# Reordering the first pair of each group of seven-product matmul pairs, and splitting two SiLU blocks earlier, in a hybrid encoder layer

## The chip, the cores and the metric

The kernel runs on one core of one Trainium2 chip, as one program in one launch. The metric is the device time of an execution in microseconds (us), the median over several executions. The engines are TensorE (PE, matmuls, with its weight loads shown as PEld), VectorE (DVE), ScalarE (ACT), GpSimd (POOL) and SyncE (SP, which issues the weight loads). They run side by side and each takes its own instructions in order.

## What is computed

One layer of a streaming encoder on 640 token rows: a prompt of 512 and 8 samples of 16. Everything is float32.

```
z = x @ w_in                      # columns: xa | ya | glu | q | gates (3 x 1024)
out_a = (rg_lru(conv4(xa)) * gelu(ya)) @ proj_a
out_b = silu(layer_norm(conv31(glu))) @ proj_b
out_c = cross_attention(q, mem_k, mem_v) @ proj_c
merged = g0 * out_a + g1 * out_b + g2 * out_c        # g = sigmoid(gates + b_gate)
x = layer_norm(alpha * x + merged @ w_out)
ffn = (silu(x @ w_ffn_gate) * (x @ w_ffn_up)) @ w_ffn_down   # 2816 wide
x = layer_norm(alpha * x + ffn)
```

## The kernel before

A float32 product is made of three matmuls on rounded operands: every operand is split into a high part (an ACT copy into the rounded type) and a low part (a DVE subtraction of the high part from the original), and hi x hi, hi x lo and lo x hi are added. The function `split` (line 206) is this for one operand. The transposed activations stand in two big tiles, `xh` and `xl`, as eight blocks of 128 features by 640 tokens.

Two groups of weight columns are multiplied by a scheme of seven products in place of eight (Winograd's variant of Strassen's): the eleven-pair FFN part (gate and up projections, all but their first 256 columns) and the last 1024 gate columns. A pair is a 1024 x 256 weight block. Its x operand is cut into four quarters, by feature half and token half: "11", "12", "21", "22" (line 1382). Four sums of quarters are needed too: s1 = 21 + 22, s2 = s1 - 11, s3 = 11 - 21, s4 = 12 - s2. `sums_stream` (line 1386) makes them once for each group, in two blocks of two features each: four adds `xh + xl`, four sums of those, and then the splits of s2, s3, s1, s4. The first group (the gates) writes s1's split in place over quarter 21 of `xh` and `xl`, which no product reads.

`Pair` (line 1429) makes four sums of weight blocks, t1 to t4, on DVE. `seven` (line 1464) issues the products in the order of the table `PRODUCTS` (line 1459): m1 (quarter 11), m6 (s2), m2 (quarter 12), m7 (s3), m5 (s1), m4 (quarter 22), m3 (s4). Each is 12 matmuls of 128 x 320. Four PSUM tiles hold them: m1 and m2 add up in tile x, m6 and m7 in y, m5 and m3 in z, m4 is alone in w. After m1 ACT copies x out; after m6, DVE adds y to that copy; after m7, again; and the four results of a pair are put out after m2, m5, m4 and m3. A product that continues a tile can start only when the earlier value has been read out of it.

The program is recorded step by step (line 1842). A step stands for one product or another block of matmuls. Its weights are rounded (`prep_hi` on ACT, `prep_lo` on DVE) two steps ahead. Before its matmuls its `before` hook runs. After the first part of its matmuls, `advance` lets the side streams (attention, convolutions, the recurrence, the sums) issue instructions as far as a table of prices says that ACT and DVE are free; then pending evacuations are issued. `finish("sums0")` and `finish("sums1")`, the hooks of the second product of each group's first pair (lines 1504 and 1699), issue what is left of the sums.

The down projection follows the FFN pairs. Its left operand is `hT`, 22 blocks of 128 features (the SiLU blocks). `split_h(k)` (line 1701) rounds block k; `before_down` (line 1709), the hook of the first down step, splits blocks 0 and 1, and each step k then splits block k + 2. The weights come in blocks of 1 MB, two at a time; a load starts when the last low half of an older block is made (`Load.take`, line 226).

Of the kernel before, what the change touches and what calls it, by code (L numbers as in the profile page):

```python
# [11 lines left out]
OP = mybir.AluOpType  # L12
# [126 lines left out]
def f32(x):  # L139
    return x.bitcast(F32)  # L140
# [3 lines left out]
def trunk(ctx, tc, x_prompt, x_sample, mem_prompt, state_conv_a, state_lru, state_conv_b, cache_mem_k, cache_mem_v,  # L144
# [171 lines left out]
    def flush():  # L316
        while pending:
            pending.pop(0)()
# [1066 lines left out]

    def sums_stream(in_place=None):

        for n, (t0, k0) in QUARTERS.items():
            quarters[n] = tuple([x[:, k0 + k, t0:t0 + HT] for k in range(half)] for x in (xh, xl))
        parts = {n: ([], []) for n in ("s1", "s2", "s3", "s4")}  # L1390
        last = []
        for i in range(0, half, 2):
            a = {}
            for n, (t0, k0) in QUARTERS.items():
                a[n] = get([128, 2, HT])
                V.tensor_tensor(a[n], *(f32(x[:, k0 + i:k0 + i + 2, t0:t0 + HT]) for x in (xh, xl)), op=OP.add)
                yield "v"
            for out, p, q, op in (("22", "21", "22", OP.add), ("21", "11", "21", OP.subtract),
                                  ("11", "22", "11", OP.subtract), ("12", "12", "11", OP.subtract)):
                V.tensor_tensor(a[out], a[p], a[q], op=op)  # L1400
                yield "v"
            for n, q in (("s2", "11"), ("s3", "21"), ("s1", "22"), ("s4", "12")):
                if n == "s1" and in_place is not None:
                    last.append((i, a[q]))
                    continue
                hi, lo = get([128, 2, HT], F32R), get([128, 2, HT], F32R)
                split(hi, lo, a[q])
                free(a[q])
                sums.extend((hi, lo))
                for to, y in zip(parts[n], (hi, lo)):  # L1410
                    to.extend(y[:, k] for k in range(2))
                yield 1
        if in_place is not None:
            while not in_place():
                yield None
            for i, x in last:
                hi, lo = (y[:, i:i + 2, HT:] for y in (xh, xl))
                split(hi, lo, x)
                free(x)
                yield 1  # L1420
            parts["s1"] = quarters.pop("21")
        quarters.update(parts)

    def sums_over():
        flush()
# [3 lines left out]
    class Pair:  # L1429
# [21 lines left out]
            self.add("t4", "t2", "21", OP.subtract)  # L1451

        def drop(self, n):
            if n in self.t and n != "t2":
                free(self.t.pop(n))
                if n == "t4":
                    free(self.t.pop("t2"))

    PRODUCTS = (("m1", "x", True, "11", "11"), ("m6", "y", True, "s2", "t2"), ("m2", "x", False, "12", "21"),
                ("m7", "y", False, "s3", "t3"), ("m5", "z", True, "s1", "t1"), ("m4", "w", True, "22", "t4"),  # L1460
                ("m3", "z", False, "s4", "22"))
    parity = [0]

    def seven(pair, put, following, begin=None):

        acc, tmp = {}, {}

        def after(n, p):
            if n == "m1":
                tmp["a"], tmp["b"] = get([128, 2, HT]), get([128, 2, HT])  # L1470
                copy(tmp["a"][:, 0], p)
            elif n == "m6":
                V.tensor_tensor(tmp["a"][:, 1], tmp["a"][:, 0], p, op=OP.add)
            elif n == "m2":
                put(0, 0, p, None, None)
            elif n == "m7":
                V.tensor_tensor(tmp["b"][:, 0], tmp["a"][:, 0], p, op=OP.add)
            elif n == "m5":
                put(1, 1, p, tmp["b"][:, 0], OP.add)
            elif n == "m4":  # L1480
                put(0, 1, p, tmp["b"][:, 0], OP.subtract)
                free(tmp["b"])
            else:
                put(1, 0, p, tmp["a"][:, 1], OP.add)
                free(tmp["a"])

        for i, (n, u, opens, xn, wn) in enumerate(PRODUCTS):
            def mm(w, u=u, opens=opens, xn=xn):
                if opens:
                    acc[u] = pu(1)[0][:, :HT]  # L1490
                p = acc[u]
                hi, lo = w
                xhi, xlo = quarters[xn]
                for k in range(half):
                    P.matmul(p, hi[:, k], xhi[k], start=opens and k == 0, stop=False, skip_group_check=not opens)
                    P.matmul(p, hi[:, k], xlo[k], start=False, stop=False, skip_group_check=not opens)
                yield
                for k in range(half):
                    P.matmul(p, lo[:, k], xhi[k], start=False, stop=k == half - 1, skip_group_check=not opens)
                yield  # L1500

            before = None
            if i == 1:
                before = begin
            elif following and i == 2:
                before = following.sums_1
            elif following and i == 3:
# [6 lines left out]
    def pair_steps(pairs, begin=None):  # L1514

        early = steps[-2]
        assert early.before is None
        early.before = lambda: (pairs[0][0].sums_1(), pairs[0][0].sums_2())
        for i, (pair, put) in enumerate(pairs):
            seven(pair, put, pairs[i + 1][0] if i + 1 < len(pairs) else None, begin if i == 0 else None)  # L1520
# [32 lines left out]
    for j in range(KD):  # L1553
# [1 line left out]
    first["pairs"] = len(steps)  # L1555
    pair_steps([(Pair(w_load(w_in, C_G + 128 * j, 7)),
                 through(AF.Sigmoid, lambda i, j=j: slot_of(gates, (0, j + i)), bias=lambda i, j=j: pa[:, j + i, 8:9]))
                for j in range(0, KD, 2)], lambda: finish("sums0"))
    proj_steps(0, proj_a, 8, aT, lambda: (sums_over(), finish("lru", "a")))


# [133 lines left out]
    for m2 in range(2, KF, 2):  # L1695
        pairs.append((Pair(w_load(w_ffn_gate, m2 * 128, 7)),
                      through(AF.Silu, lambda i, m2=m2: slot_of(hT, m2 + i))))
        pairs.append((Pair(w_load(w_ffn_up, m2 * 128, 7)), times(m2)))
    pair_steps(pairs, lambda: finish("sums1"))

    def split_h(k):
        if k < KF:
# [5 lines left out]

    def before_down():
        sums_over()  # L1710
        for k in range(2):
            split_h(k)
        r = one.tile([128, 5, D], F32, name="xres", tag="xh")
        for t in range(5):
            G.dma_start(r[:, t], scratch["x1"][t * 128:(t + 1) * 128, :])
            res[t] = [r[:, t, c * 512:(c + 1) * 512] for c in range(2)]
        g = one.tile([128, 2, D], F32, name="gb2", tag="xl")
        for i, z in enumerate((ln2_g, ln2_b)):
            G.dma_start(g[:, i], bass.AP(tensor=z.tensor, offset=z.offset, ap=[[0, 128], [1, D]]))
        gb["2"] = [[g[:, i, c * 512:(c + 1) * 512] for c in range(2)] for i in range(2)]  # L1720
# [176 lines left out]
```

## Time and profile before

| what | value |
|---|---|
| median of 3 executions | 1102.43 us (1102.43 to 1102.51) |
| the profiled execution: its time, its span | 1102.82 us, 1101.1 us |
| PE busy, weight loads busy | 97%, 91% of the span |
| DVE, ACT, POOL busy | 73%, 44%, 15% |
| mean granted TensorE clock | 0.989 of full speed |

The span runs from the first to the last instruction of the core; the time of the execution is 1.7 us longer. Busy shares are averages over stages with different limits. A row of a timeline gives the start in us from the span's start, the duration, the engine, the operation, output tile, input tiles, their shapes, how many equal instructions in a row stand behind it, and in brackets how long the engine stood idle before it and who ended that. `s` is any slot of the pool (640 floats in each of 128 partitions), `wr` a raw weight block, `wh` and `wl` two buffers that hold rounded weights (in a pair step each holds both halves of one product's weights, by turns), `pu` and `pv` PSUM tiles.

### The profile page before, as it was taken

The page shows a single profiled execution, that of the slowest core. Times are in us where ns is not written, and L with a number is a line of the kernel's source. Part 1 is how long each engine was busy: PE and PEld are TensorE (multiplying, and loading weights), DVE is VectorE, ACT ScalarE, POOL GpSimd, SP SyncE. Part 2 cuts the span into 40 slices and gives each one's busy share as a digit, 9 for nine tenths or more (in the row PEclk, how much of TensorE's full clock was granted, in tenths as well). Part 3 has the DMA queues.
Part 4 walks back from the last instruction along what each step waited for, and adds up shares of the span by engine and source line. Part 5 has one row for each costly group of instructions (what it writes and reads, how often), then busy time and mean ns, then how long its engine had stood idle before and what let it go on. Part 6 is the DMA issues. An engine that isn't in the chain of part 4 may idle for free.

```text
span 1101.1 us, 16991 instructions
## 1 busy us (share of the span) xinstructions
PE 1064.1 (97%) x6827; PEld 1007.0 (91%) x6827; DVE 799.0 (73%) x1333; ACT 486.9 (44%) x861; POOL 165.0 (15%) x185
## 2 busy tenths in 40 slices
PE   8799898998999999999999999999999999999997
PEld 6699898997999999999999889899999999788886
DVE  6929898994465865699655579888887887544775
ACT  4532545445648346646423023444444443344341
POOL 3623323556200000010001120000000000100111
PEclk9999999998999999999999999999999999999999
DMA  9732123353313113212325431222233222734481
GB/s 339 252 95 78 39 67 96 118 154 94 118 39 96 59 58 115 78 44 77 115 78 172 148 120 59 71 82 78 77 95 97 77 77 86 278 115 132 165 294 39
DMA packets 80334, 123.11 MB, mean 112 GB/s; under 512 B 4075, under 2 KB 59371, under 8 KB 80256
## 3 DMA queue, kind: packets, MB, share of 16 engines
q1 hardware_dynamic: 73168, 100.36, 27.6%
q0 software_dynamic: 7088, 21.68, 6.3%
q8 instruction: 53, 0.87, 0.3%
q14 instruction: 25, 0.20, 0.1%
HBM read 112.41 MB, written 9.61 MB: 111 GB/s over the span
## 4 chain that ended last, share of the span: by engine, by line
PE 76%; DVE 14%; ACT 3%; issue 2%; POOL 2%; DMA 1%; SPq 0%; DVEq 0%; ACTq 0%; POOLq 0%
PE pu L64 67%; DVE s L64 12%; PE pv L64 9%; ACT s L64 2%; DVE wl L64 1%; ACT L64 1%; POOL s L540 1%; POOL s L541 1%; DMA s<-in_w_mem_k 0%; ACT wh L64 0%; DMA wr<-in_w_ffn_down 0%; DMA s<-in_x_prompt 0%; DVE xres L64 0%; DVE xl L64 0%; DVE mx L64 0%
## 5 line engine op out<-in xcount | busy, mean ns | idle before, releaser
L64 PE MATMUL pu<-xh,wh 128*128 128x320 f32 x1040 | 251.7, 314 | 4.6 <-ACT s L64 3.0
L64 PE MATMUL pu<-xh,wl 128*128 128x320 f32 x1040 | 246.9, 310 | 0.0
L64 ACT ACTIVATE wh<-wr 128x1024 fp32r<-128x1024 f32 (+1 forms) x149 | 135.1, 908 | 236.8 <-PE pu L64 139.0
L64 PE MATMUL pu<-xl,wh 128*128 128x320 f32 x888 | 219.4, 310 | 0.0
L64 PE MATMUL pu<-s,wh 128*128 128x320 f32 x1064 | 185.7, 310 | 1.6 <-ACT s L64 1.1
L64 PEld LDWEIGHTS pu<-xh,wh 128*128 128x128 f32 x1040 | 177.6, 189 | 9.4 <-ACT s L64 3.8
L64 PEld LDWEIGHTS pu<-xh,wl 128*128 128x128 f32 x1040 | 177.5, 189 | 0.0
L64 DVE TENSOR_TENSOR s<-s,s 128x640 fp32r<-128x640 f32 (+4 forms) x176 | 124.1, 723 | 62.4 <-ACT s L64 57.2
L64 PEld LDWEIGHTS pu<-s,wh 128*128 128x128 f32 x1064 | 163.4, 188 | 3.0 <-ACT s L64 1.7
L64 DVE TENSOR_TENSOR wl<-wr,wh 128x1024 fp32r<-128x1024 f32 (+1 forms) x100 | 114.1, 1142 | 67.6 <-ACT wh L64 67.6
L64 PEld LDWEIGHTS pu<-xl,wh 128*128 128x128 f32 x888 | 154.0, 189 | 0.6 <-DVE xl L64 0.6
L64 PE MATMUL pu<-s,wl 128*128 128x320 f32 x808 | 148.6, 311 | 2.8 <-ACT s L64 1.6
L64 DVE TENSOR_TENSOR s<-s,pu 128x320 f32<-128x320 f32 x186 | 87.8, 484 | 79.9 <-PE pu L64 77.1
L64 DVE SCALAR_TENSOR_TENSOR s<-s,pb,s 128x511 f32<-128x511 f32 (+14 forms) x240 | 130.1, 614 | 7.8 <-ACT s L64 7.8
L64 PEld LDWEIGHTS pu<-s,wl 128*128 128x128 f32 x808 | 126.6, 189 | 3.8 <-DVE s L64 1.9
L64 ACT ACTIVATE s<-s 128x640 fp32r<-128x640 f32 (+4 forms) x144 | 86.9, 628 | 97.2 <-DVE s L64 94.7
L64 PE MATMUL pu<-wh,s 128*128 128x512 f32 (+1 forms) x396 | 117.6, 390 | 3.0 <-ACT s L64 2.6
L64 PEld LDWEIGHTS pu<-wh,s 128*128 128x128 f32 x396 | 73.8, 191 | 18.2 <-ACT s L64 2.9
L64 ACT ACTIVATE s<-pu 128x320 f32<-128x320 f32 (+2 forms) x90 | 36.7, 442 | 75.5 <-PE pu L64 75.5
L64 PE MATMUL pu<-wl,s 128*128 128x512 f32 (+1 forms) x198 | 63.3, 391 | 1.5 <-POOL wl L305 0.8
L305 POOL TENSOR_TENSOR wl<-wr,wh 128x1024 fp32r<-128x1024 f32 x13 | 44.4, 3414 | 83.1 <-ACT wh L64 70.3
L64 PE MATMUL pv<-wh,s 128*128 128x512 f32 (+1 forms) x152 | 48.7, 368 | 0.4 <-DVE xres L64 0.4
(139 smaller groups left out, 1241.6 us busy)
## 6 DMA issues: line engine op xcount, KB each, us to landing
wr<-in_w_in SPq DMA_DIRECT2D x26, 1024.0 KB, 5.2
wr<-in_w_ffn_down SPq DMA_DIRECT2D x19, 1024.0 KB, 5.0
wr<-in_w_ffn_gate SPq DMA_DIRECT2D x11, 1024.0 KB, 5.4
wr<-in_w_ffn_up SPq DMA_DIRECT2D x11, 1024.0 KB, 5.4
s<-in_cache_mem_k POOLq DMA_DIRECT2D x16, 256.0 KB, 7.4
s<-in_cache_mem_v POOLq DMA_DIRECT2D x16, 256.0 KB, 6.9
wr<-in_proj_a SPq DMA_DIRECT2D x4, 1024.0 KB
wr<-in_w_out SPq DMA_DIRECT2D x4, 1024.0 KB, 5.9
```

Of the source, the lines that this page charges most:

```text
L64: return f(*a, **k)
L305: self.eng.tensor_tensor(l, x, f32(h), op=OP.subtract)
L540: G.tensor_tensor(y[1], y[1], g[1], op=OP.mult)
L541: G.tensor_tensor(y[1], y[1], b[1], op=OP.add)
```

## The change

The sums are made in another order, and the first pair of each group takes its products in another order; the other pairs are as before. The first pair's order is now m1, m4, m2, m6, m7, m5, m3, so that the three products on plain quarters come first. `sums_stream` first makes everything of s2, s3 and s1 for both blocks, then the splits of s2, s3 and (where not in place) s1, and only then the two adds and sums that lead to s4, and its splits. In place of one `finish` at the second product, each product on a sum has a hook `sum_there` that flushes the pending evacuations and then issues the stream until that sum is there. The result of m4 is put out after m7, since it needs what m7 completes. The sums t1 to t4 of the second pair's weights are made together, before m2. The two `split_h` calls of `before_down` move to the hooks of the third and the fourth step of the last FFN pair (m2 and m7).

```diff
     def sums_stream(in_place=None):
...
+        blocks = range(0, half, 2)
+        for i in blocks:
+            whole("22", i)
+            whole("21", i)
+            yield "v"
+            mix("22", "21", "22", i, OP.add)
+            whole("11", i)
+            yield "v"
+            mix("21", "11", "21", i)
+            mix("11", "22", "11", i)
+            yield "v"
+        yield from part("s2", "11", True)
+        yield from part("s3", "21")
+        if in_place is None:
+            yield from part("s1", "22")
+        for i in blocks:
+            whole("12", i)
+            yield "v"
+            mix("12", "12", "11", i)
+            free(a.pop(("11", i)))
+            yield "v"
+        yield from part("s4", "12")
...
+    def sum_there(n):
+
+        flush()
+        for item in list(streams):
+            while item[0][:4] == "sums" and n not in quarters:
+                try:
+                    next(item[1])
+                except StopIteration:
+                    streams.remove(item)
+                    break
+        assert n in quarters
...
             elif n == "m7":
                 V.tensor_tensor(tmp["b"][:, 0], tmp["a"][:, 0], p, op=OP.add)
+                if late:
+                    fourth(late.pop())
...
             elif n == "m4":
-                put(0, 1, p, tmp["b"][:, 0], OP.subtract)
+                if first:
+                    late.append(p)
+                else:
+                    fourth(p)
...
-        for i, (n, u, opens, xn, wn) in enumerate(PRODUCTS):
+        products = [PRODUCTS[i] for i in ((0, 5, 2, 1, 3, 4, 6) if first else range(7))]
+        for i, (n, u, opens, xn, wn) in enumerate(products):
...
-            if i == 1:
-                before = begin
+            if first and xn[0] == "s":
+                before = lambda xn=xn: sum_there(xn)
+            elif first and i == 2 and following:
+                before = lambda: (following.sums_1(), following.sums_2())
...
-    pair_steps(pairs, lambda: finish("sums1"))
+    pair_steps(pairs)
+    for k in range(2):
+        assert steps[-5 + k].before is None
+        steps[-5 + k].before = lambda k=k: split_h(k)
...
     def before_down():
         sums_over()
-        for k in range(2):
-            split_h(k)
```

How the change moves instructions, at three places. On DVE in the first pair of the gates, the rows before ran from the first block of weight sums for the second pair to the read of m7 (`s_308` is the copy of m1 and then m1 + m6, `s_309` that plus m7; `s_310` to `s_313` are weight sums; `s_221` and `s_306` belong to the recurrence's output):

```order
L64 TENSOR_TENSOR s_306_5199<-s_216_3391,s_305_5198 128x640
L64 TENSOR_TENSOR s_310_5246<-wr 128x512
L64 TENSOR_TENSOR s_311_5248<-s_310_5246,wr 128x512
L64 TENSOR_TENSOR s_308_5226<-s_308_5226,pu 128x320
L64 TENSOR_TENSOR wh<-s_293_5062,wh 128x512
L64 TENSOR_TENSOR s_312_5266<-wr 128x512
L64 TENSOR_TENSOR s_313_5268<-s_311_5248,wr 128x512
L64 TENSOR_TENSOR wl<-s_294_5064,wl 128x512
```

and now:

```order
L64 TENSOR_TENSOR s_310_5246<-wr 128x512
L64 TENSOR_TENSOR s_311_5248<-s_310_5246,wr 128x512
L64 TENSOR_TENSOR s_312_5250<-wr 128x512
L64 TENSOR_TENSOR s_313_5252<-s_311_5248,wr 128x512
L64 TENSOR_TENSOR wh<-s_287_5052,wh 128x512
L64 TENSOR_TENSOR wl<-s_289_5056,wl 128x512
L64 TENSOR_TENSOR s_308_5236<-s_308_5236,pu 128x320
```

The read of m6 (`s_308<-s_308,pu`) stands behind two more weight sums and the low halves of two products' weights.

On DVE in the first FFN pair before (`s_417`, `s_423` to `s_429` the second block of s4's sum and of the four splits, `s_420` the copy of m1):

```order
L64 TENSOR_TENSOR s_417_7012<-s_417_7012,s_416_6983 128x640
L64 TENSOR_TENSOR s_423_7046<-s_416_6983,s_422_7045 128x640
L64 TENSOR_TENSOR s_425_7050<-s_418_7014,s_424_7049 128x640
L64 TENSOR_TENSOR s_427_7054<-s_419_7027,s_426_7053 128x640
L64 TENSOR_TENSOR s_429_7058<-s_417_7012,s_428_7057 128x640
L64 TENSOR_TENSOR wl<-s_403_6903,wl 128x512
L64 TENSOR_TENSOR s_430_7077<-wr 128x512
L64 TENSOR_TENSOR s_431_7079<-s_430_7077,wr 128x512
L64 TENSOR_TENSOR s_420_7039<-s_420_7039,pu 128x320
```

and now, from the read of m7 on (`s_421` is what m7 completes, `s_426` the result of m4, `s_428` the low half of s1's second block, `s_429` and `s_431` the two blocks of s4's sum, `s_430` the result of m5, `s_433` and `s_435` the low halves of s4):

```order
L64 TENSOR_TENSOR s_421_7050<-s_420_7049,pu 128x320
L64 TENSOR_TENSOR s_426_7082<-s_421_7050,pu 128x320
L64 TENSOR_TENSOR s_428_7122<-s_401_6880,s_427_7121 128x640
L64 TENSOR_TENSOR s_429_7125<-xh,xl 128x640
L64 TENSOR_TENSOR wl<-wr,wl 128x512
L64 TENSOR_TENSOR s_430_7143<-s_421_7050,pu 128x320
L64 TENSOR_TENSOR s_429_7125<-s_429_7125,s_400_6849 128x640
L64 TENSOR_TENSOR s_431_7147<-xh,xl 128x640
L64 TENSOR_TENSOR s_431_7147<-s_431_7147,s_409_6969 128x640
L64 TENSOR_TENSOR s_433_7151<-s_429_7125,s_432_7150 128x640
L64 TENSOR_TENSOR s_435_7155<-s_431_7147,s_434_7154 128x640
```

All splits stood ahead of the read of m6; now one split of s1 stands behind the reads of m7 and m4, and five instructions for s4 behind the read of m5.

On ACT at the end of the FFN pairs, as a difference (`s_402`/`s_403` and `s_407`/`s_408` are SiLU blocks 0 and 1, `s_434`/`s_426` block 2, each named before and now; `wh<-wr 128x1024` rounds a down weight block):

```order
 L64 ACTIVATE wl<-s_585_9500 128x512
+L64 ACTIVATE s_591_9613<-s_403_6884 128x640
 L64 ACTIVATE wh<-s_586_9502 128x512
+L64 ACTIVATE s_593_9633<-s_408_6924 128x640
 L64 ACTIVATE wl<-wr 128x512
 L64 ACTIVATE wh<-wr 128x1024 x3
-L64 ACTIVATE s_594_9709<-s_402_6882 128x640
-L64 ACTIVATE s_596_9713<-s_407_6923 128x640
-L64 ACTIVATE s_598_9726<-s_434_7109 128x640
+L64 ACTIVATE s_598_9726<-s_426_7082 128x640
```

The copies of blocks 0 and 1 stood behind the rounding of three down weight blocks and now stand ahead of it.

## Rows read from the trace of the kernel before

**Rows 1.** The page: PE's busy time, and the chain that ended last by engine.

```profile
PE 1064.1 (97%) x6827; PEld 1007.0 (91%) x6827; DVE 799.0 (73%) x1333; ACT 486.9 (44%) x861; POOL 165.0 (15%) x185
...
PE 76%; DVE 14%; ACT 3%; issue 2%; POOL 2%; DMA 1%; SPq 0%; DVEq 0%; ACTq 0%; POOLq 0%
```

**Rows 2.** The longest of PE's waits over the whole span: us in total, times, the longest.

```profile
PE pu L64 <- ACT s L64: 8.3, 5, 2.6
```

**Rows 3.** PE's timeline in the first two gate pairs: m6 and m7 of the first, m6 and m7 of the second.

```profile
494.68 1.92 PE L64 MATMUL pu<-s,wl 128*128 128x320 f32 x12
...
499.04 2.03 PE L64 MATMUL pu<-s,wl 128*128 128x320 f32 x12 [0.68 <-DVE s L64]
...
507.99 1.92 PE L64 MATMUL pu<-s,wh 128*128 128x320 f32 x12
...
511.51 1.92 PE L64 MATMUL pu<-s,wh 128*128 128x320 f32 x12
```

**Rows 4.** DVE's timeline in the first gate pair: the low halves in place, the read of m6, two weight sums.

```profile
493.76 1.56 DVE L64 TENSOR_TENSOR xl<-s,xh 128x640 fp32r<-128x640 f32 x2 [1.95 <-ACT xh L64]
...
498.50 0.48 DVE L64 TENSOR_TENSOR s<-s,pu 128x320 f32<-128x320 f32 x1
...
499.50 0.68 DVE L64 TENSOR_TENSOR s<-wr 128x512 f32<-128x512 f32 x1
500.11 0.68 DVE L64 TENSOR_TENSOR s<-s,wr 128x512 f32<-128x512 f32 x1
```

**Rows 5.** PE's timeline: a stop in an earlier stage, and then the first FFN pair from m1's first matmul, with m6 in three pieces, m7, and the first matmul of the second pair.

```profile
428.32 1.12 PE L64 MATMUL pu<-s,wh 128*128 128x320 f32 x4 [1.06 <-ACT s L64]
...
686.55 0.31 PE L64 MATMUL pu<-xh,wh 128*128 128x320 f32 x1
...
688.31 0.75 PE L64 MATMUL pu<-s,wl 128*128 128x320 f32 x4
690.66 0.42 PE L64 MATMUL pu<-s,wl 128*128 128x320 f32 x1 [1.60 <-ACT s L64]
691.52 2.24 PE L64 MATMUL pu<-s,wl 128*128 128x320 f32 x7 [0.44 <-DVE s L64]
...
696.05 2.03 PE L64 MATMUL pu<-s,wl 128*128 128x320 f32 x12
...
703.20 0.31 PE L64 MATMUL pu<-xh,wl 128*128 128x320 f32 x1
```

**Rows 6.** DVE's timeline around the first FFN pair: four adds, three sums that each wait for the one before, and the read of m6.

```profile
666.19 3.02 DVE L64 TENSOR_TENSOR s<-xh,xl 128x640 f32<-128x640 f32 x4
669.24 2.55 DVE L64 TENSOR_TENSOR s<-s,s 128x640 f32<-128x640 f32 x3
...
695.51 0.48 DVE L64 TENSOR_TENSOR s<-s,pu 128x320 f32<-128x320 f32 x1
```

**Rows 7.** ACT's timeline: the high halves of a block's four sums; and, in the last pairs, a SiLU and the weight copy behind it.

```profile
689.87 2.62 ACT L64 ACTIVATE s<-s 128x640 fp32r<-128x640 f32 x4 [0.93 <-DVE s L64]
...
922.52 0.47 ACT L64 ACTIVATE s<-s 128x320 f32<-128x320 f32 x1 [2.57 <-DVE s L64]
922.89 0.61 ACT L64 ACTIVATE wh<-s 128x512 fp32r<-128x512 f32 x1
```

**Rows 8.** Stretches of the span: from:to, length, busy us (and instructions) of PE, PEld, DVE, ACT and POOL, then the granted TensorE clock, the DMA share and GB/s.

```profile
425.00:430.00 5.00, 3.94 (x25) 3.45 (x24) 0.34 (x1) 4.98 (x8) 0.00 (x0) 1.00 0.00 1
...
691.40:694.70 3.30, 3.18 (x12) 3.19 (x13) 3.30 (x6) 2.13 (x4) 0.00 (x0) 0.50 0.00 0
...
940.50:943.80 3.30, 3.30 (x8) 2.62 (x9) 3.30 (x4) 1.15 (x2) 0.28 (x1) 0.50 0.85 292
```

**Rows 9.** PE's timeline at the start of the down projection: the last pair's m5 and m3, the first down matmuls, and those of the second step.

```profile
932.38 1.92 PE L64 MATMUL pu<-s,wl 128*128 128x320 f32 x12
...
935.89 1.93 PE L64 MATMUL pu<-s,wl 128*128 128x320 f32 x12
940.45 1.22 PE L64 MATMUL pu<-wh,s 128*128 128x512 f32 x2 [2.63 <-ACT s L64]
...
946.28 0.62 PE L64 MATMUL pu<-wh,s 128*128 128x512 f32 x2
...
947.19 1.07 PE L64 MATMUL pu<-wh,s 128*128 128x512 f32 x4
```

**Rows 10.** DVE's and then ACT's timeline in the last pair and at the start of the down projection.

```profile
929.12 0.49 DVE L64 TENSOR_TENSOR s<-s,pu 128x320 f32<-128x320 f32 x1 [1.36 <-PE pu L64]
...
932.98 0.68 DVE L64 TENSOR_TENSOR wl<-wr,wl 128x512 fp32r<-128x512 f32 x1
934.34 0.49 DVE L64 TENSOR_TENSOR s<-s,pu 128x320 f32<-128x320 f32 x1 [0.67 <-PE pu L64]
...
935.27 1.22 DVE L64 TENSOR_TENSOR wl<-wr,wh 128x1024 fp32r<-128x1024 f32 x1
...
938.46 0.48 DVE L64 TENSOR_TENSOR s<-s,pu 128x320 f32<-128x320 f32 x1
...
932.57 1.06 ACT L64 ACTIVATE wh<-wr 128x1024 fp32r<-128x1024 f32 x1 [2.35 <-PE pu L64]
938.72 1.06 ACT L64 ACTIVATE wh<-wr 128x1024 fp32r<-128x1024 f32 x1 [5.08 <-DMA wr<-in_w_ffn_down]
939.68 1.98 ACT L64 ACTIVATE s<-s 128x640 fp32r<-128x640 f32 x3
```

More of the change, by code (lines that the diff above doesn't have):

```diff
@@ L1386, in sums_stream @@
     def sums_stream(in_place=None):
+        quarters.clear()
         for n, (t0, k0) in QUARTERS.items():
             quarters[n] = tuple([x[:, k0 + k, t0:t0 + HT] for k in range(half)] for x in (xh, xl))
[L1390 to L1396, printed above, removed]
-                yield "v"
[L1398 to L1412, printed above, removed]
@@ new lines, in sums_stream, with whole, mix, part @@
+        a = {}
+        def whole(n, i):
+            t0, k0 = QUARTERS[n]
+            a[n, i] = get([128, 2, HT])
+            V.tensor_tensor(a[n, i], *(f32(x[:, k0 + i:k0 + i + 2, t0:t0 + HT]) for x in (xh, xl)), op=OP.add)
+        def mix(out, p, q, i, op=OP.subtract):
+            V.tensor_tensor(a[out, i], a[p, i], a[q, i], op=op)
+        def part(n, q, keep=False):
+            at = [], []
+            for i in blocks:
+                hi, lo = get([128, 2, HT], F32R), get([128, 2, HT], F32R)
+                split(hi, lo, a[q, i])
+                if not keep:
+                    free(a.pop((q, i)))
+                sums.extend((hi, lo))
+                for to, y in zip(at, (hi, lo)):
+                    to.extend(y[:, k] for k in range(2))
+                yield "v"
+            quarters[n] = at
@@ new lines, in sums_stream @@
+        blocks = range(0, half, 2)
[13 more added lines that the diff above has]
+            yield from part("s1", "22")
+        for i in blocks:
+            whole("12", i)
[3 more added lines that the diff above has]
+            yield "v"
@@ L1415, in sums_stream @@
                 yield None
[L1416 to L1419, printed above, removed]
+            for i in blocks:
+                split(*(y[:, i:i + 2, HT:] for y in (xh, xl)), a["22", i])
+                free(a.pop(("22", i)))
                 yield 1
-            parts["s1"] = quarters.pop("21")
-        quarters.update(parts)
+            quarters["s1"] = quarters.pop("21")
+    def sum_there(n):
[8 more added lines that the diff above has]
+        assert n in quarters
     def sums_over():
@@ L1453, in drop @@
         def drop(self, n):
-            if n in self.t and n != "t2":
+            if n in self.t:
                 free(self.t.pop(n))
-                if n == "t4":
-                    free(self.t.pop("t2"))
     PRODUCTS = (("m1", "x", True, "11", "11"), ("m6", "y", True, "s2", "t2"), ("m2", "x", False, "12", "21"),
@@ L1462, in trunk, with seven, fourth @@
     parity = [0]
-    def seven(pair, put, following, begin=None):
-        acc, tmp = {}, {}
+    def seven(pair, put, following, first=False):
+        acc, tmp, late = {}, {}, []
+        def fourth(p):
+            put(0, 1, p, tmp["b"][:, 0], OP.subtract)
         def after(n, p):
@@ L1480, in after @@
             elif n == "m4":
-                put(0, 1, p, tmp["b"][:, 0], OP.subtract)
+                if first:
+                    late.append(p)
+                else:
+                    fourth(p)
+            else:
                 free(tmp["b"])
-            else:
                 put(1, 0, p, tmp["a"][:, 1], OP.add)
                 free(tmp["a"])
-        for i, (n, u, opens, xn, wn) in enumerate(PRODUCTS):
+        products = [PRODUCTS[i] for i in ((0, 5, 2, 1, 3, 4, 6) if first else range(7))]
+        for i, (n, u, opens, xn, wn) in enumerate(products):
             def mm(w, u=u, opens=opens, xn=xn):
@@ L1512, in seven, with pair_steps @@
             parity[0] += 1
-    def pair_steps(pairs, begin=None):
+    def pair_steps(pairs):
         early = steps[-2]
@@ L1519, in pair_steps @@
         for i, (pair, put) in enumerate(pairs):
-            seven(pair, put, pairs[i + 1][0] if i + 1 < len(pairs) else None, begin if i == 0 else None)
+            seven(pair, put, pairs[i + 1][0] if i + 1 < len(pairs) else None, i == 0)
     def w_load(w, col, users):
@@ L1557, in trunk @@
                  through(AF.Sigmoid, lambda i, j=j: slot_of(gates, (0, j + i)), bias=lambda i, j=j: pa[:, j + i, 8:9]))
-                for j in range(0, KD, 2)], lambda: finish("sums0"))
+                for j in range(0, KD, 2)])
     proj_steps(0, proj_a, 8, aT, lambda: (sums_over(), finish("lru", "a")))
```

## Prediction

> **What bounds the kernel now.** I read the page first: TensorE (PE) is busy for 97% of the span, and 76% of the chain that ended last is PE itself, 14% DVE [rows 1]. So whatever keeps PE fed costs nothing, and only places where PE stands still can move the time. The list of waits says which: PE's longest wait for ACT is 2.6 us, of 8.3 us for ACT's copies into slots in all [rows 2]. Then I looked at the three places that the change touches, on PE's timeline. Between stops a product of a pair (12 matmuls) starts every 1.76 us: 507.99 to 511.51 is two of them [rows 3]. I call the three places A, B and C.
>
> A, first pair of the gates: from the start of m6 at 494.68 to the start of the second pair's m6 at 507.99 seven products take 13.31 us instead of 7 x 1.76 = 12.32. It **loses 0.99**, nearly all at 499.04, where m7 had to wait until DVE had read m6's sum out of the same PSUM tile [rows 3, 4].
>
> B, first FFN pair: m1 starts at 686.55 and the second pair's m1 at 703.20. That is 16.65 for seven products, so **4.33 is lost**. m6 stood 1.60 for the ACT copy of s2's second block and 0.44 for its DVE half, because DVE had all sums of the first block in front of it. Then the granted clock was 0.50 from 691.4 to 694.7, and m7 waited for DVE's read of m6 [rows 5, 6, 8].
>
> C, start of the down projection: the last m3 starts at 935.89 and is issued by 937.65, yet the first down matmul starts at 940.45. It waits for ACT's copy of the first SiLU block at 939.68, which stands behind the rounding of the third weight block, which waits until 938.72 for its DMA [rows 9, 10]. That is 2.80. Then the clock is 0.50 again [rows 8]: the first 18 matmuls, 940.45 to 946.28, take 5.83, where the rate after it (four from 946.28 to 947.19, 0.91) makes 4.09, so 1.74 more. **C loses 4.54.**
>
> **The change, step by step.** No arithmetic is added or removed: the same seven products, sums and splits, in another order. SP and POOL issue the same transfers in the same order, so no queue is passed.
>
> *C.* The copies of blocks 0 and 1 (2 x 0.7 on ACT, 2 x 0.83 on DVE) go ahead of the last pair's m2 and m7. ACT has 2.35 us free before 932.57 and DVE 1.36 before 929.12 and 0.67 before 934.34 [rows 10], so they fit beside PE. DVE's reads of that pair may be some 0.4 late, and the load that waits for the last weight half at 932.98 with them; it is needed only for the third block, 8.2 us of matmuls after 937.65. The first weight block's low half is done at 935.27 + 1.22 = 936.49 [rows 10], before PE asks. What is late next is the fourth PSUM tile, read at 938.46 + 0.48 [rows 10], about when the second token tile needs it. So the stop goes and with it the low clock: **gain 4.5** (4.0 if that read holds PE up).
>
> *A and B, the two handoffs.* In the new order m7 follows m6 directly, and m3 follows m5, and each pair of them adds into one PSUM tile. m7 may start only when DVE has read m6's sum. A product's last result is there 1.92 after its start, 0.16 after the next could start [rows 3]; DVE starts 0.04 later (932.38 + 1.92 = 934.30, read at 934.34 [rows 9, 10]), takes 0.48, and PE starts 0.06 after it (498.98 to 499.04 [rows 3, 4]). That makes **0.74 a handoff**, two in each first pair. The trace has such a handoff only where DVE was late, at 499.04, so 0.74 is its floor. The Trainium skill, Perfetto Trace Analysis, section Matmuls under Optimizing Tensor Performance, says that groups of matmuls should rotate through PSUM banks so that reading one out overlaps the next group, and that one accumulation group stays in one bank. It speaks against this order: by it the four handoffs cost 3.0; were they hidden as the old order hides them, the sum below would be 3.0 lower. Row 499.04 sides with the Trainium skill here.
>
> *A.* DVE's work before m6's read is now longer by two weight sums and two low halves, about 2.4 at a pitch of 0.61 [rows 4], but the read is due two products (3.52) later, at about 500.1. If the in-place low halves start at 493.76 as before, DVE gets there at 500.8, 0.7 late; if the sums, which have fewer instructions that wait for the one right before, are done earlier, it is in time. I take 0.3 (bounds 0 and 0.7). A now loses 2 x 0.74 + 0.3 = 1.8: **0.8 slower**.
>
> *B.* m1, m4, m2 need nothing of the sums. m6 is due 5.3 after m1. By the order DVE had 17 of the sums' 128x640 instructions in front of the last evacuation ahead of this pair, and has 17 now; but now they are all of s2 and s3 and half of s1, so these are there about when m1 starts, and the old stop at m6 goes. But s1's second block, and nearly all of s4, are asked for only right before m5 and m3, with a forced flush that puts the read of the product just run ahead of them. I follow the chain from m1 = 0 by these durations: read 0.48, a dependent one 0.05 later, SiLU 0.47 of which 0.37 holds the next, 128x640 copy 0.7 (four take 2.62, three 1.98), 128x640 sum or low half 0.83 at a pitch of 0.73 (four take 3.02, two 1.56) [rows 4, 6, 7, 10].
> m6 ends at 7.04, m7 starts at 7.78 and ends at 9.54. m5 issues its first four matmuls by 10.13. DVE reads m7 until 10.22 and m4 until 10.75, ACT does SiLU from 10.78 and copies s1's block from 11.15 to 11.85; PE resumes at 11.9 (1.8 lost), stops again until DVE's low half at 12.75 (0.7 lost), and m5 ends at 13.8. DVE reads m5 until 14.5, takes the first 12-sum until 15.25, ACT copies until 16.0: m3 starts 2.2 late. Its second matmul needs two more sums and a low half on DVE, to 17.6: 1.45 lost, and 0.2 at the last block. The pair lasts about 19.5, so B loses 0.74 + 2.5 + 3.9 = 7.1 for 4.33: **2.8 slower**, between 2.4 and 3.2 as the pitches go.
> Two 128x640 instructions of which one waits for the other are 0.86 apart (2.55 for three, less 0.83), others 0.73 [rows 6], and two such pairs lie on the chain. The Trainium skill, VectorE: DVE Perf Modes, section The DRAIN you can't avoid, says that a semaphore between two DVE instructions costs nothing extra. By it the chain and the sum would be 0.3 lower; I keep the row.
>
> *The clock.* After 1.60 + 0.44 of standing at B, and after 2.63 at C, the granted clock was 0.50 over the 3.3 us that the view was asked for; after 1.06 at 428 it stayed at 1.00 [rows 5, 8, 9]. B's new stops are longer than either, so the lower level follows. In C's case it cost 1.74; where PE stands anyway it costs nothing. Bounds 0 and 2 x 1.74. I take one visible stretch, **1.7 slower**, as at C.
>
> **Sum.** -4.5 + 0.8 + 2.8 + 1.7 = +0.8 us. The profiled execution took 1102.82, so 1103.6 in it; the median of the three runs is 0.39 below it, 1102.43, so the forecast is **1103.2**: no difference that this kernel's measurement can tell, which needs about 0.2%, 2.2 us.
>
> **Rivals.**
> - *The clock stays up at B.* Its new stops come in four pieces, none over 2.3. Then the sum is -0.9: 1101.5. For it: at 428 a shorter stop left it up. Against: 691.4 to 694.7. The Trainium skill, TensorE: Matmul & The Clock Gate, section on why this matters for kernels, would leave the clock up after pieces this short; by it the answer is this case.
> - *Slower: the low clock holds twice.* The stops of m5 and m3 together are over twice C's. If the lower level comes in two stretches in which PE works, m3's end and most of the second pair run at half rate: 1.74 more, 1105.0. It decides if the granted clock is 0.50 in two stretches after m5's first matmuls, both with PE busy.
> - *Faster: the late pieces of s1 and s4 do not hold PE.* Then B loses only its handoffs, 1.5 for 4.33, with no low clock: 0.8 - 2.8 - 4.5 = -6.5, 1095.9. For it: the stream may run ahead. Against: the order puts s4's sums behind the read of m5, and m5 is 1.76 long.
> - *C gains nothing*, because another input of the first down matmul is as late: 4.5 more, 1107.7. Against: 936.49 above.
>
> **How the numbers follow.** Forecast 0.55, clock up 0.20, low clock twice 0.11, late pieces hidden 0.08, no gain at C 0.06. Faster by over 0.2% (below 1100.2) is the fourth case alone, 0.08. Slower (above 1104.6) is the third and the last, 0.17; within is 0.75. The range takes the first three: down from 1101.5 by the lower bounds of A and B, to 1100.8, and up to 1105.2; it leaves out the last two and the tails.
>
> **What would show it.** Right: no PE wait over 0.3 at the start of the down projection and full clock there; in each first pair two waits for DVE of 0.5 to 0.9 at m7 and m3; at B waits for ACT of about 1.7 and 2.1 in m5 and m3 with DVE waits behind them, and a clock of 0.50 after them. Wrong: a first FFN pair shorter than 16.6 us, a stop still at the first down matmul, or PE waits in pairs after the first.

## The result, and the profile of the changed kernel

The changed kernel takes **1105.21 us** (median of 15 executions, 1103.74 to 1106.08) beside 1102.43 for the kernel before (15, 1101.55 to 1102.86): a ratio of 1.0025, interval 1.0018 to 1.0033. That is 2.8 us slower, at the upper end of the range (1100.8 to 1105.2) and over the 2.2 that the text called measurable. The number can only be understood with one more: three executions, the profiled one (1103.96) among them, have a mean granted clock of 0.992 and lie at 1103.74 to 1104.45, one has 0.991 (1104.84), and the other eleven have 0.988 or 0.989 and lie at 1104.95 to 1106.08.

The wait of PE that grew most, from 3.2 us in 5 times to 7.1 in 9 (us in total, times, the longest):

```profile
PE pu L64 <- DVE s L64: 7.1, 9, 1.2
```

Of the 3.9 more, 2.8 are at A and B: the handoffs and what stands behind them. The rest is one wait of 1.1 at 156 us, in a stage that the change does not touch; a second profile of the same kernel (e3 below) does not have it.

PE's timeline at A (m6, m7, the first matmul of m5, m3, the first of the second pair), beside [rows 3]:

```profile
498.37 1.92 PE L64 MATMUL pu<-s,wl 128*128 128x320 f32 x12
501.53 1.99 PE L64 MATMUL pu<-s,wh 128*128 128x320 f32 x12 [1.24 <-DVE s L64]
503.36 0.31 PE L64 MATMUL pu<-xh,wl 128*128 128x320 f32 x1
...
505.96 1.99 PE L64 MATMUL pu<-s,wh 128*128 128x320 f32 x12 [0.67 <-DVE s L64]
507.79 0.31 PE L64 MATMUL pu<-xh,wl 128*128 128x320 f32 x1
```

DVE's timeline there, beside [rows 4]: the low halves in place, the read of m6, the read of m5.

```profile
493.75 1.56 DVE L64 TENSOR_TENSOR xl<-s,xh 128x640 fp32r<-128x640 f32 x2 [1.95 <-ACT xh L64]
...
500.91 0.48 DVE L64 TENSOR_TENSOR s<-s,pu 128x320 f32<-128x320 f32 x1
...
505.32 0.49 DVE L64 TENSOR_TENSOR s<-s,pu 128x320 f32<-128x320 f32 x1 [0.15 <-PE pu L64]
```

m7 starts 3.16 after m6, 1.40 late; m3 2.60 after m5, 0.84 late; behind each the next product is 0.07 late (1.83 for 1.76). From m6 to the second pair four products take 9.42, 7.04 without stops: **A loses 2.38**, for 0.99 before. The low halves start at the same time as before (493.75), so DVE reaches m6's read at 500.91, 0.58 later than m6's result allowed (498.37 + 1.92 + 0.04).

PE's timeline at B (m1's first matmul, m6, m7, m5 in three pieces, m3 in two, the first matmul of the second pair), beside [rows 5]:

```profile
688.10 0.31 PE L64 MATMUL pu<-xh,wh 128*128 128x320 f32 x1
...
693.38 1.92 PE L64 MATMUL pu<-s,wl 128*128 128x320 f32 x12
695.97 2.00 PE L64 MATMUL pu<-s,wh 128*128 128x320 f32 x12 [0.67 <-DVE s L64]
697.81 0.75 PE L64 MATMUL pu<-s,wl 128*128 128x320 f32 x4
700.20 0.41 PE L64 MATMUL pu<-s,wl 128*128 128x320 f32 x1 [1.64 <-ACT s L64]
701.06 1.29 PE L64 MATMUL pu<-s,wl 128*128 128x320 f32 x7 [0.45 <-DVE s L64]
704.43 0.63 PE L64 MATMUL pu<-s,wh 128*128 128x320 f32 x1 [2.08 <-ACT s L64]
705.99 3.30 PE L64 MATMUL pu<-s,wh 128*128 128x320 f32 x11 [0.93 <-DVE s L64]
709.09 0.45 PE L64 MATMUL pu<-xh,wl 128*128 128x320 f32 x1
```

The two inputs that m3 waits for: DVE's read of m5, then the first sum of s4, the second add and the last three; and ACT's first copy for s4.

```profile
702.39 0.49 DVE L64 TENSOR_TENSOR s<-s,pu 128x320 f32<-128x320 f32 x1
702.79 0.82 DVE L64 TENSOR_TENSOR s<-s,s 128x640 f32<-128x640 f32 x1
703.53 0.82 DVE L64 TENSOR_TENSOR s<-xh,xl 128x640 f32<-128x640 f32 x1
704.38 2.45 DVE L64 TENSOR_TENSOR s<-s,s 128x640 f32<-128x640 f32 x3
```

```profile
703.64 0.74 ACT L64 ACTIVATE s<-s 128x640 fp32r<-128x640 f32 x1 [0.27 <-DVE s L64]
```

From 688.10 to 709.09 seven products take 20.99: **B loses 8.67**, for 4.33 before. In pieces: handoff 0.83 + 0.08, m5 1.80 (ACT) and 0.71 (DVE), 2.34 until m3, 1.41 in m3 (DVE), and 1.49 because m3's last 11 matmuls run at half rate (3.10 for 1.62). C and the clock, in PE's timeline (the last m3, the first down matmuls, and those after 18) and in stretches of the span as in [rows 8]:

```profile
941.56 1.92 PE L64 MATMUL pu<-s,wl 128*128 128x320 f32 x12
943.32 0.63 PE L64 MATMUL pu<-wh,s 128*128 128x512 f32 x2
...
947.42 0.62 PE L64 MATMUL pu<-wh,s 128*128 128x512 f32 x2
```

```profile
706.00:709.30 3.30, 3.30 (x12) 3.30 (x13) 1.43 (x2) 0.49 (x1) 0.00 (x0) 0.50 0.00 0
709.50:712.40 2.90, 2.90 (x22) 2.90 (x21) 2.41 (x5) 2.19 (x5) 0.00 (x0) 1.00 0.00 0
943.30:947.40 4.10, 4.10 (x20) 3.40 (x19) 3.04 (x5) 1.69 (x2) 2.64 (x6) 1.00 1.02 325
```

The down projection starts 1.76 after m3, and its first 18 matmuls take 4.10 at a clock of 1.00: **C loses nothing**, for 4.54. The sum is +1.39 + 4.34 - 4.54 = +1.2; the spans differ by 1.1 and the two profiled executions by 1.14.

### The profile page after: what moved, and what is told of

It reads as the page before. It is cut to its first block, busy times and chain, and to the rows that moved or that the text cites. A ratio compares the mean times of both kernels' runs of the same rounds, so it can differ in the third digit from the quotient of the medians.

```text
span 1102.2 us, 16991 instructions
## 1 busy us (share of the span) xinstructions
PE 1061.4 (96%) x6827; PEld 1004.2 (91%) x6827; DVE 799.2 (73%) x1333; ACT 487.2 (44%) x861; POOL 165.0 (15%) x185
## 4 chain that ended last, share of the span: by engine, by line
PE 73%; DVE 10%; ACT 2%; issue 1%; POOL 0%; DVEq 0%; ACTq 0%; POOLq 0%
PE pu L64 65%; DVE s L64 9%; PE pv L64 8%; ACT s L64 2%; DVE xres L64 0%; DVE wl L64 0%; ACT L64 0%; DVE mx L64 0%; ACT wh L64 0%; DVE xl L64 0%; POOL s L855 0%; DVE wh L64 0%; DVEq L1937 0%; ACT xh L64 0%; DVE st L64 0%
## 5 line engine op out<-in xcount | busy, mean ns | idle before, releaser
L64 PE MATMUL pu<-s,wh 128*128 128x320 f32 x1076 | 189.6, 312 | 7.2 <-DVE s L64 4.1
L64 PEld LDWEIGHTS pu<-s,wh 128*128 128x128 f32 x1076 | 166.2, 189 | 9.8 <-ACT s L64 4.1
L64 PE MATMUL pu<-s,wl 128*128 128x320 f32 x796 | 145.4, 309 | 2.1 <-ACT s L64 1.6
L64 PEld LDWEIGHTS pu<-s,wl 128*128 128x128 f32 x796 | 123.8, 188 | 2.6 <-ACT s L64 1.9
```

What stands on the lines that cost most here:

```text
L64: return f(*a, **k)
```

## The experiments

The last three columns are what the profiled execution loses: at A and B the time from the first pair's m1 to the second pair's m6 less eight products of 1.76; at C the stop ahead of the first down matmul and what the first 18 take over 4.10. (B of the changed kernel is 8.82 in this count, which reaches one product further than the 8.67 above.) The time ahead of A differs between executions too: the profiled ones of e1 and e8 reach A 1.3 and 1.5 sooner than that of before, already in stages that no edit touches. The columns leave this out, the medians do not.

| kernel | median us | ratio (interval) | A | B | C |
|---|---|---|---|---|---|
| before | 1102.43 | | 0.99 | 4.33 | 4.5 |
| changed, first profile | 1105.21 | 1.0025 (1.0018 to 1.0033) | 2.38 | 8.82 | 0 |
| e1, SiLU move alone | 1097.73 | 0.9955 (0.9943 to 0.9968) | 1.01 | 4.33 | 0 |
| e2, orders alone | 1107.32 | 1.0049 (1.0033 to 1.0064) | 2.41 | 8.85 | 3.0 |
| e3, changed again | 1104.88 | 1.0024 (1.0015 to 1.0033) | 2.40 | 10.19 | 0 |
| e4, m7 in its own tile | 1102.09 | 0.9995 (0.9986 to 1.0004) | 1.24 | 8.48 | 0 |
| e5, s1 and s4 early (m5 unread, see there) | 1099.24 | 0.9973 (0.9962 to 0.9984) | 2.35 | 4.07 | 0 |
| e6, products as before | 1101.38 | 0.9991 (0.9982 to 1.0000) | 1.99 | 7.21 | 0 |
| e7, DVE reordered | 1097.41 | 0.9963 (0.9950 to 0.9975) | 0.37 | 5.98 | 0 |
| e8, adds on POOL | 1096.84 | 0.9953 (0.9939 to 0.9966) | 2.66 | 1.48 | 0 |
| e9, on POOL in the FFN alone | 1094.14 | 0.9923 (0.9910 to 0.9935) | 0.14 | 1.49 | 0 |
| e10, e5 with m5 read first | 1100.48 | 0.9980 (0.9971 to 0.9989) | 2.40 | 5.28 | 0 |
| e11, all pairs | 1145.44 | 1.0388 (1.0372 to 1.0404) | | | |

Ratios are to runs of the kernel before on the same chip. The theory: the order of DVE's queue and the four handoffs set A and B, the SiLU move alone sets C, and a low clock behind B's stops is added. Rivals: B is bounded by DVE's whole work, wherever it stands; or the clock alone makes the difference.

**e1** takes the kernel before and moves only the two splits.

```diff
+    for k in range(2):
...
+        steps[-5 + k].before = lambda k=k: split_h(k)
...
     def before_down():
         sums_over()
-        for k in range(2):
-            split_h(k)
```

> Kernel before with only the two SiLU blocks moved to the last pair; products and sums as before. If the stop at the start of the down projection and the low clock behind it are all that the move takes away, 4.54 us go: 1097.9, a ratio of 0.9959, first down matmul right behind the last product, the granted clock 1.00 there, and A and B as before (0.99 and 4.33 lost). If the stop only turns into another (a late read of the fourth PSUM tile, a weight half), under 2.8 us go: above 1099.6.

Measured 1097.73, 4.6 less than the kernel before beside it (1102.31): the first case. PE's timeline at B and the clock there:

```profile
689.35 0.41 PE L64 MATMUL pu<-s,wl 128*128 128x320 f32 x1 [1.61 <-ACT s L64]
690.21 1.29 PE L64 MATMUL pu<-s,wl 128*128 128x320 f32 x7 [0.45 <-DVE s L64]
694.74 2.02 PE L64 MATMUL pu<-s,wl 128*128 128x320 f32 x12 [1.48 <-DVE s L64]
```

```profile
691.30:694.70 3.40, 1.96 (x14) 1.69 (x12) 3.37 (x7) 2.32 (x5) 0.00 (x0) 1.00 0.00 0
```

The stops in m6 are those of before to 0.01 [rows 5], yet the clock stayed at 1.00 here and was 0.50 there [rows 8]. And B loses 4.33 in both: before, the half rate only filled time in which m7 would have waited for DVE's read.

**e2** is the change with the splits put back (the opposite edit).

> The change without the move of the two SiLU blocks: only the order of the sums and of the first pairs. If the three places add up, it is the changed kernel plus 4.5: 1109.7, a ratio of 1.0066, with A and B as in the changed kernel (2.4 and 8.7 lost) and C as before (2.8 of standing, 1.7 of low clock). If the longer stop at B and the stop at C share the low clock, it is nearer 1108.

Measured 1107.32, 2.4 below the first case (executions 1106.79 to 1110.02; the longest has a mean clock of 0.986, the other three 0.991 or 0.992). A and B are the changed kernel's; C has the stop but not the low clock:

```profile
946.59 0.73 PE L64 MATMUL pu<-wh,s 128*128 128x512 f32 x2 [2.72 <-ACT s L64]
```

```profile
946.40:950.00 3.60, 3.41 (x15) 2.78 (x16) 3.43 (x4) 1.40 (x3) 0.43 (x1) 1.00 0.96 355
```

The stop ahead is 2.72, before it was 2.63 with 0.50 behind it. So the places add up in their stops, and the low clock comes or not. The median is nearer to the second case; but the execution at 1110.02, with its lower mean clock, lies where the first case has it, so the low clock at B does not seem to keep it away at C.

**e3** is the changed kernel, unedited.

> The changed kernel once more, for an execution whose mean granted clock is 0.988: 12 of its 15 executions have it, while the profiled one has 0.992 and is 1.25 us shorter than the median. If the rival with two low stretches holds, the profile of such an execution has the clock at 0.50 in more places in which PE works, at A or at B (first pairs longer than 9.42 from m6 and 20.99), and all else alike; its time is then about 1105.2. If the 1.25 come from elsewhere (start, end, transfers), A, B and C are as in the first profile.

Its profiled execution has 0.988. Two stretches at B, and PE's rows of the second pair's first matmul and its m6:

```profile
706.00:709.40 3.40, 3.05 (x11) 3.05 (x12) 1.72 (x3) 0.85 (x2) 0.00 (x0) 0.50 0.00 0
709.50:712.40 2.90, 2.90 (x13) 2.90 (x13) 2.26 (x4) 0.99 (x2) 0.00 (x0) 0.50 0.00 0
```

```profile
709.45 0.47 PE L64 MATMUL pu<-xh,wl 128*128 128x320 f32 x1
...
712.57 1.62 PE L64 MATMUL pu<-s,wh 128*128 128x320 f32 x10
```

The stops of B are the same to 0.01, and the clock stays at 0.50 through the second pair's m1: 3.12 for 1.91 in the first profile. B loses 10.19. That is the rival with two stretches.

The mean of 0.988 is not B's alone. In e3 the clock is 0.50 also near 40 and near 139 us, where the first profile has 1.00:

```profile
139.10:142.30 3.20, 3.20 (x14) 3.20 (x14) 3.20 (x4) 1.71 (x4) 3.00 (x1) 0.50 0.00 0
```

These two cost little, since A starts only 0.18 later than in the first profile. The profile of e6 below has both of them as well, and at B the clock is 0.50 only until 709; its mean is 0.990. So a mean of 0.988, which nine of the 15 executions have (the expectation counts 12), points at the longer stretch at B.

**e4** gives m7 a PSUM tile of its own.

```diff
-                V.tensor_tensor(tmp["b"][:, 0], tmp["a"][:, 0], p, op=OP.add)
+                V.tensor_tensor(tmp["b"][:, 0], tmp["a"][:, 1 if first else 0], p, op=OP.add)
...
+            if first and n == "m7":
+                u, opens = "y7", True
```

> The change with one edit: in the first pairs m7 opens a PSUM tile of its own, and DVE adds it to m1 + m6 in place of m1. If m7 stands because m6 must be read out of the same tile, the stops ahead of m7 go (1.40 + 0.07 at A, 0.91 at B), the reads behind them come earlier by as much, and s1's and s4's late pieces with them: 2.4 us less, 1102.8, ratio 1.0003; m3's stop for m5 stays. If m7 stands for s3 or for its weights, the stops stay: 1105.2.

Measured 1102.09, 2.8 below the changed kernel beside it. PE at A (m6, m7, m3), then at B (m6, m7):

```profile
497.62 1.92 PE L64 MATMUL pu<-s,wl 128*128 128x320 f32 x12
499.37 1.92 PE L64 MATMUL pu<-s,wh 128*128 128x320 f32 x12
...
504.06 2.00 PE L64 MATMUL pu<-s,wh 128*128 128x320 f32 x12 [1.01 <-ACT wh L64]
```

```profile
691.51 1.92 PE L64 MATMUL pu<-s,wl 128*128 128x320 f32 x12
693.27 1.92 PE L64 MATMUL pu<-s,wh 128*128 128x320 f32 x12
```

m7 follows m6 after 1.75 and 1.76: both stops ahead of m7 were the shared tile. At A only 1.16 of 1.47 came back, because m3 now waits 1.01 for rounded weights, where it stood 0.67 for DVE. B loses 1.71 less than in e3, of which 0.91 is the handoff; most of the other 0.8 is a low clock that ends earlier (the second pair's m1 takes 2.47, in e3 3.12), so the 2.8 are not the tile alone.

**e5** forces the sums earlier, **e10** does the same and keeps the read of m5 ahead of m3 (the lists for "s1" and "s4" are e10's; in e5 both are empty). In e5 the flush ahead of m3 is gone with its hook, so m3's first eight matmuls add into m5's tile before m5 has been read: e5 does not compute the layer, and e10 is the version that counts.

```diff
-                before = lambda xn=xn: sum_there(xn)
+                before = lambda xn=xn: [sum_there(s) for s in {'s2': ('s2', 's3', 's1'), 's3': ('s4',), 's1': ('s1',), 's4': ('s4',)}[xn]]
```

> The change with its forced sums earlier: the hook of m6 issues s2, s3 and s1, that of m7 issues s4; products as in the change. If m5 and m3 stand because s1's second block and s4 are asked for too late, their ACT stops (1.64 and 2.08) and the DVE stops behind them go; DVE reads m6 about 1.5 later and m5's result about 1.2 later for it, so B loses some 5 in place of 7.2 before any low clock: 1101.7, and 1100 where the clock stays at 1.00. If DVE's work as a whole bounds B, the stops only move from m5 and m3 to m7 and m3: 1105.

> The version with s1 and s4 forced earlier, with the flush that reads m5 out ahead of m3 put back (in the first form m3's first eight matmuls were issued ahead of that read, so that a quarter of the result took in a part of m3). All 12 matmuls of m3 now wait for the read of m5 that DVE made at 703.2 there, where only the last four waited: 8 x 0.147 = 1.2 more than 1099.2, 1100.4, and 1102 where that longer stop lowers the clock. By the theory that DVE's whole work bounds B: 1104 to 1105.

Measured 1099.24 and 1100.48. PE at B in e10 (m7, m5, m3), then the stretch behind m7's stop in e10 and in e5:

```profile
697.47 2.71 PE L64 MATMUL pu<-s,wh 128*128 128x320 f32 x12 [2.08 <-DVE s L64]
699.99 2.79 PE L64 MATMUL pu<-s,wl 128*128 128x320 f32 x12
703.96 1.99 PE L64 MATMUL pu<-s,wh 128*128 128x320 f32 x12 [1.19 <-ACT wh L64]
```

```profile
698.60:701.80 3.20, 3.20 (x13) 3.20 (x13) 3.09 (x5) 1.50 (x3) 0.00 (x0) 0.50 0.00 0
```

```profile
698.40:701.60 3.20, 3.20 (x24) 3.20 (x23) 3.09 (x5) 1.53 (x3) 0.00 (x0) 1.00 0.00 0
```

The ACT stops for s1 and s4 in m5 and m3 are gone; m7 stands 2.08 for DVE's read of m6 instead. B loses 4.07 and 5.28, 1.21 apart as worked out, though what m3 waits for last in e10 is its rounded weights, 0.14 after DVE's read of m5 has ended. So DVE's work as a whole does not bound B: in e10 the same instructions in another order lose 3.5 less than in the first profile of the change, 4.9 less than in e3. In e10 the clock was 0.50 behind that 2.08, in e5 it stayed at 1.00 behind a 2.08.

**e6** keeps all but the order of the products.

```diff
...
-        products = [PRODUCTS[i] for i in ((0, 5, 2, 1, 3, 4, 6) if first else range(7))]
+        products = [PRODUCTS[i] for i in range(7)]
```

(The lines left out put m4's result out at once, since m7 stands ahead of it again.)

> The change with the products of the first pairs in the order of before (m1, m6, m2, m7, m5, m4, m3), its sums, hooks and the SiLU move kept. If two products in a row on one PSUM tile cost 0.9 each, all four handoffs go and with them the lateness at A: A loses about 1.0 as before, B the late pieces of s4 alone, some 4.5 to 5 with what low clock falls in: 1101.5. If the handoffs were only a part of one wait for DVE (the late pieces grow by what they give back), it stays at 1104 to 1105.

Measured 1101.38. The total came out, its parts only by half: B loses 7.21 with a low clock, but A still 1.99, where I expected 1.0. PE's m7 at A (m6 starts at 495.00):

```profile
500.41 2.02 PE L64 MATMUL pu<-s,wl 128*128 128x320 f32 x12 [1.73 <-DVE s L64]
```

m7 stands 1.73 for DVE's read of m6, with m2 between them. The second pair's four weight sums, all issued ahead of m2 by the change, stand in front of that read (two of them did before, and DVE read m6 at 498.50 [rows 4], here at 499.88). e7, which among other edits splits them again, is rid of it; that edit alone is not tested.

**e7, e8, e9** are meant to beat both. e7 is e6 with s2 and s3 forced ahead of m6, s1 and s4 ahead of m7, t3 and t2 made ahead of m7, t1 and t4 ahead of m3. e8 is e7 with s4's two adds on POOL, e9 has them there only in the FFN group. First e7's edit of the hooks, then e9's of the adds:

```diff
+                before = lambda xn=xn: [sum_there(s) for s in {'s2': ('s2', 's3'), 's3': ('s3', 's1', 's4'), 's1': (), 's4': ()}[xn]]
...
+            if first and following and i in (3, 6):
+                before = lambda i=i, b=before: (b and b(), i == 3 and following.sums_1(), i == 6 and following.sums_2())
```

```diff
+            whole("12", i, nc.gpsimd if in_place is None else V)
...
         for i in blocks:
-            whole("12", i)
-            yield "v"
```

> A version meant to beat both: the products in the order of before, the sums in the new order, s2 and s3 forced ahead of m6, s1 and s4 ahead of m7, the sums of the second pair's weights split again and later (t3 and t2 ahead of m7, t1 and t4 ahead of m3), and the SiLU move. By the theory that the order of DVE's queue sets A and B: nothing lost at A, some 3.3 at B in two pieces, nothing at C: 1095.9, or 1097.6 with one low stretch. If DVE's whole work bounds B: about 4.3 lost there, 1097 to 1099.

> As the version before it, with the two adds that lead to s4 (xh + xl of quarter 12) on POOL, which stands idle there, issued with the first adds. If DVE's whole work bounds B, 1.5 less on DVE is 1.5 less at B: 1094.4. If POOL and DVE slow each other down while both add, part or all of it is lost: 1095 to 1097.

> As the version with the adds on POOL, but on POOL in the FFN group alone; in the gates they stay on DVE. With POOL's add at 472.02 in the gates two DVE adds took 3.73 in place of 1.55, and that version lost 1.93 at A, which the one without POOL did not. If DVE's slowing beside POOL is the cause, A loses nothing, B some 1.0, C nothing: 1.9 less, 1094.9. If A's loss came from the execution and not from POOL: 1096.8 again.

Measured 1097.41, 1096.84 and **1094.14** (1093.61 to 1094.49), 0.77% under the kernel before. In e7 PE still stood 2.08 at B in m4, with the clock at 0.50 behind it:

```profile
698.29 0.85 PE L64 MATMUL pu<-xh,wl 128*128 128x320 f32 x4 [2.08 <-DVE wl L64]
```

With 0.64 ahead of m3 that is nearly all of its standing at B, less than either case of its expectation (3.3 or 4.3); most of the rest of the 5.98 is half rate. Its profiled execution is the longest of five (1099.48; the others 1096.00 to 1099.27). In e8 B loses 1.48, but A 2.66. In the gates DVE's add and POOL's:

```profile
471.29 3.00 DVE L64 TENSOR_TENSOR s<-xh,xl 128x640 f32<-128x640 f32 x1
```

```profile
472.02 1.57 POOL L1396 TENSOR_TENSOR s<-xh,xl 128x640 f32<-128x640 f32 x1
```

e9 has no add of POOL beside an add of DVE, and both places are nearly clean: A loses 0.14, so e8's loss there came with POOL's add in the gates. Its PE at B (the stops in m4 and ahead of m3):

```profile
695.27 0.85 PE L64 MATMUL pu<-xh,wl 128*128 128x320 f32 x4 [0.35 <-DVE wl L64]
696.76 2.00 PE L64 MATMUL pu<-s,wh 128*128 128x320 f32 x12 [0.64 <-DVE s L64]
```

**e11** uses the new order in every pair but the last of a group.

```diff
-            seven(pair, put, pairs[i + 1][0] if i + 1 < len(pairs) else None, i == 0)
+            seven(pair, put, pairs[i + 1][0] if i + 1 < len(pairs) else None, i < len(pairs) - 1)
```

> The changed kernel with the new order in every pair but the last of each group: 20 more pairs, 40 more handoffs, no sums in them. If a handoff costs PE what it does at B's m7 (0.83 and 0.08 behind it), 40 x 0.91 = 36 more: 1141. If later pairs hide them (DVE and ACT have less to do there), under 1120; if DVE comes late to them as at A (0.66 more at every other one), 1154.

The gates have four pairs and the FFN part has twenty (ten of each projection, not eleven pairs in all), so 2 + 18 pairs are new. Measured 1145.44, 40.6 over the changed kernel (e3), so 1.01 for each of 40 handoffs, a tenth more than B's m7 gave. PE's waits for DVE, and one later pair (m6, m7, m5; its m3 at 770.93 stands 0.67 too):

```profile
PE pu L64 <- DVE s L64: 36.6, 48, 1.3
```

```profile
763.90 1.93 PE L64 MATMUL pu<-s,wl 128*128 128x320 f32 x12
766.50 1.99 PE L64 MATMUL pu<-s,wh 128*128 128x320 f32 x12 [0.67 <-DVE s L64]
768.33 1.92 PE L64 MATMUL pu<-s,wl 128*128 128x320 f32 x12
```

Even where DVE has room and no sums are due, a handoff is not hidden: 2.60 from start to start, and 1.83 to the next. Ahead of m3 PE stands 0.96 in every other later FFN pair and 1.18 in the later gate pairs, so DVE comes late there as well, and that is most of the tenth.

## Why the prediction was right, and where it was not

- *C, gain 4.5.* Right: 4.54 in the trace, 4.6 alone (e1). The stop and the low clock went together, and nothing became late in their place.
- *The handoffs, 0.74 each.* Right in kind, a fifth too small: 0.83 or 0.84 and 0.07 or 0.08 behind, 0.91; at A DVE began m5's read 0.04 after the result, as worked out (503.36 + 1.92, read at 505.32), and PE followed that read after 0.15, not 0.06. e4 shows that it is the shared tile, e11 that none of 40 is hidden. The Trainium skill, Perfetto Trace Analysis, section Matmuls, has independent groups of matmuls rotate through PSUM banks; e4, where m7 becomes such a group and follows m6 after 1.75, agrees.
- *A, 0.8 slower.* Too small: 1.39. About half of the difference are the two handoffs, the other half is DVE's lateness at m6's read, taken as 0.3 between 0 and 0.7; it was 0.58. The low halves in place start when they did before (493.75), so the branch that the prediction itself priced at 0.7 was the one to take.
- *B, 2.8 slower before the clock.* The chain held piece by piece: 1.8 and 0.7 in m5 (1.80, 0.71), 2.2 until m3 (2.34), 1.45 in it (1.41). Only the 0.2 at the last block is not seen; there PE was at half rate. The 0.86 for a DVE instruction that waits for the one before, which I kept against the Trainium skill (VectorE: DVE Perf Modes, The DRAIN you can't avoid, which found no extra cost of a semaphore in a row of copies), showed again: 0.85 from 703.53 to 704.38, and 0.74 from 702.79 to 703.53.
- *The clock, one visible stretch, 1.7.* In the profiled execution so: 1.49. This is the step that failed for the median. In e3 the low level held through the next product as well and cost 1.37 more, about the 1.25 between the first profile and the median. With the traces' numbers the median is 1102.43 - 4.54 + 1.39 + 4.34 + 1.37 = 1105.0, measured 1105.21: the rival "the low clock holds twice", which I gave 0.11 and priced at 1105.0. That it was that in most executions is worked out from their mean clocks; it was seen in one profile. That the median still lies at the range's upper end owes something to luck: the 1105.2 is this rival's time and 0.2 more, which the prediction does not work out, while its own forecast, no difference that can be told, was missed by 2.0.
- *What I drew the clock from did not hold.* I let the longer stop decide. In e1 the stops of B left the clock up that lowered it before, in e2 the stop of C did, and 2.08 lowered it in e10 and not in e5. A stop of this size makes the lower level possible, not certain, and the forecast should have split its chance between one and two stretches. The Trainium skill, TensorE: Matmul & The Clock Gate, in its section on why it matters for kernels, would have left the clock up here; the changed kernel's two profiles speak against that, e1 and e5 for it, and e2 at C.

## What to carry to other kernels

Products that follow each other on one PSUM tile stand for the read between them: put another product between, or give the second its own tile. An input that is asked for only right before its user, with a flush ahead of it, arrives one read and one split too late, however free the engine was earlier; force it one or two users ahead. More stops also mean more places behind which the clock may be low, and that is paid in the products that follow, unless they would have stood anyway (before, at B).

## What the runs showed of the hardware that was not expected

- The clock's answer to one and the same stop differs from execution to execution: 0.50 or 1.00 behind 1.6 + 0.45, behind 2.6 to 2.7, and behind 2.08. What decides it was not tried.
- An add of DVE on two 128x640 float32 operands took 3.00 us in place of 0.82 while POOL made one of the same shape (1.57) beside it; one case. In e9 POOL's two adds ran beside DVE subtractions that read PSUM and one SBUF tile, and those kept their time (1.28 for two). The Trainium skill, SBUF — State Buffer, section Who interferes with whom, says that a DVE instruction with at most one SBUF input, outside its 2-port modes, does not contend with GpSimd; e9's subtractions agree. DVE's add grew by 2.18 where POOL's whole add was 1.57, so more than a wait for that one instruction was lost; what the rest is stays open.
